# Hymba block on one core: raw weight buffers in two pairs, the last two tokens' rows on the tensor engine, and a rotary half swap by copies

## The chip, the cores and the metric

The kernel runs on one core of one Trainium2 chip. The metric is device time in microseconds (us), the median of several executions. One execution was also profiled; the profile gives every instruction of the engines: TensorE (PE, with its weight loads PEld), VectorE (DVE), ScalarE (ACT), GpSimd (POOL) and SyncE (SP, which here only issues DMAs).

## The reference

The model is one block on 1024 tokens of width 1024, all float32, with 16 learned meta tokens put in front (1040 tokens) and dropped at the end. Eight heads run side by side: four of an mLSTM (heads 0 to 3 in the kernel) and four of a retention (heads 4 to 7). Their mixed output is projected, a residual is added, and a gated MLP with a causal depthwise convolution follows.

```python
def reference(...):
    h = concatenate([meta, x], axis=1)
    h = h + token_mixer(rmsnorm(h, norm_mix_g), w_in, ..., w_out)
    h = h + channel_mixer(rmsnorm(h, norm_ffn_g), w_up, w_gate, ffn_conv_w, w_down)
    return rmsnorm(h, norm_final_g)[:, N_META:]

def rotary(t, pos):
    ...
    t1, t2 = t[..., : d // 2], t[..., d // 2:]
    return concatenate([t1 * cos - t2 * sin, t1 * sin + t2 * cos], axis=-1)

def token_mixer(u, w_in, ..., w_out):
    proj = up @ w_in
    (ml_q, ml_k, ml_v, ml_o, ml_i, ml_f, rt_q, rt_k, rt_v, rt_g) = split(proj)
    # mLSTM: conv + silu on q and k, a chunkwise scan with gates
    # retention: rotary on q and k, a chunkwise scan with fixed decays
    mixed = concatenate([gate(o) * head_norm(h_ml), silu(g) * head_norm(h_rt)])
    return mixed @ w_out
```

## The kernel before

**Tiling.** Activations lie with the features on the 128 partitions and the tokens along the free axis; the residual stream is eight tiles of 128 features by 1040 tokens. Each large product is done in float32r, both operands split into a high part (a rounding copy on ACT) and a low part (a subtraction on DVE), with three matmuls for each product (`mm3s`, lines 675 to 677). On top of that the large products use a Strassen-Winograd scheme with seven instead of eight block products, so the raw weights have to be added and subtracted on DVE before they are split (`quartered`, lines 361 to 385).

**Order of heads.** The mixer works on the heads in the order 4, 0, 1, 2, 3, 5, 6, 7. For each there are projection units: `q` (q and k), `o` (the output gate) and `v` (by pairs of heads, `u_vp`). PE runs these projections back to back. The scan of a head, its norm and its gating (`scan_a`, `scan_b`, `post_steps`) are put between the projection steps of the following heads.

**The order of work.** The program is dealt out in Python. `go` runs through the projection steps of a unit, and `slot` puts up to two pieces of side work from the list `side` behind each. Whether a piece is dealt depends on a running estimate of the engines' load (`load`, filled by `watch`, lines 91 to 105): side work waits while DVE or ACT is ahead of PE by more than 2.5 us. Pieces that stop at a `yield` go on at the next step (`tick`). The instruction order within the engines is then settled by the framework's list scheduler, which works from this order and its own timing estimate. Every engine, and each DMA queue, executes its instructions in order.

**Raw weight buffers.** All raw weights of the mixer pass through four tiles of 128 x 1024 (512 KB each), `raw0` to `raw3`. `job` (line 211) registers a load, and `jload` starts them strictly in the order of registration whenever one of the four slots is free:

```python
while jfreed and len(jraw) < min(len(jobs), jcap[0]):
    i = len(jraw)
    jslot[i] = jfreed.pop(0)
    ...
    nc.sync.dma_start(x[:, o:o + y.shape[1]], y)
```

Users of these slots are of two kinds. The main ones feed PE's projections: `u_load`, `u_fm` (two jobs for each `q` or `o` unit, named for instance `raw_q3a`, `raw_q3b`) and `u_vp` (four jobs). The side ones are:

- `w_unit(k)`: two blocks of `w_out` are combined by four DVE additions (lines 437 to 441) and stored to memory (line 443), as prepared operands for the output projection. Three of the eight come at the very start.
- `v_unit(p, s, r)`: the meta tokens' v, by matmuls in plain float32 on column groups of 32 (line 513, PSUM tile `pvm`), two units for each head.
- `m_unit(h)`: the output projection's contribution of the last two tokens. Those two tokens lie outside the two halves of 512 tokens that the output projection works on. For each head the two blocks of `w_out` rows (`raw_m`) are scaled by the two tokens' values `mm` (lines 414 to 418, ACT and DVE), and the result is accumulated into `accd` in memory (lines 422 and 424, the latter by an accumulating DMA of POOL). At the end (lines 1757 to 1789) `accd` is read back, the last head's share is added (line 1768), and 16 matmuls with a column of ones (line 1787, PSUM tile `pe`) sum over the partitions.
- `first_right(k)`: the mixed rows of the first eight blocks (`raw_fr`, from `mxd`), split and stored again for the first stage of the output projection (lines 479 to 485).

**Rotary.** For the retention heads (lines 919 to 932) two DVE products write each other's half of the partitions (L925, L926: 64 partitions each), a full-width product with the cosines (L928) and an addition (L929) follow. This is done for q and k and for two halves of the tokens. `gates` (lines 937 to 1026) computes the mLSTM gates once; in the side list it comes behind all four rotary pieces of head 4.

**The output projection** is the stage `mixw` (line 1241; steps "1", "65", "73", "4", "2"), with the residual's input loaded at line 1611 behind its second step. From about 742 us on the MLP follows; neither its structure nor the down projection's is touched.

Of the kernel before, what the change touches and what calls it, by code (L numbers as in the profile page):

```python
# [17 lines left out]
P = 128  # L18
# [6 lines left out]
H = 4  # L25
# [40 lines left out]
def body(ctx, tc, h_in, vecs, cst, mask_in, rot, w_v0, w_vp, w_g, w_out, w_up, w_gate, w_down, out):  # L66
# [24 lines left out]
    def watch(ins):  # L91
# [15 lines left out]
    vec = per.tile([P, V_N], F32, name="vec")  # L107
    cs = per.tile([P, C_N], F32, name="cs")
    epsc = per.tile([P, 1], F32, name="epsc")
# [16 lines left out]
    accd = [dram.tile([P, D], F32, name=f"accd{t}") for t in range(2)]  # L126
# [15 lines left out]
    mm = per.tile([P, 2 * 8, 2], F32, name="mm")  # L142
# [31 lines left out]
    AC.dma_start(vec, vecs)  # L174
# [8 lines left out]
    G.memset(gts[:, :, 0, :], 0.0)  # L183

# [20 lines left out]
    jobs = []  # L205
    jraw = {}
    jslot = {}
    jfreed = [0, 1, 2, 3]
# [5 lines left out]

    def jload():
        while jfreed and len(jraw) < min(len(jobs), jcap[0]):
            i = len(jraw)
            nm, srcs = jobs[i]
            jslot[i] = jfreed.pop(0)
            x = jraw[i] = raw_tile(nm, jslot[i])  # L220
            o = 0
            for y in srcs:
                nc.sync.dma_start(x[:, o:o + y.shape[1]], y)
                o += y.shape[1]
# [10 lines left out]

    def jfree(*ids):
        jfreed.extend(jslot[i] for i in ids)
        jload()
# [32 lines left out]
    def busy():  # L271
        return not rush[0] and max(load["DVE"], load["Activation"]) - load["PE"] > 0.5

# [67 lines left out]
    def u_load(key, *srcs):  # L341
        nm = "_".join(str(k) for k in key)
        i = job(nm, *srcs)
# [43 lines left out]
    def u_fm(kind, h, *extra):  # L387
        w = w_g[GI[kind, h]]
        nm = f"{kind}{h}"
        ja = job(nm + "a", w[:, HB:3 * HB])  # L390
        jb = job(nm + "b", w[:, 3 * HB:], w[:, :HB])
# [4 lines left out]
    def u_vp(p):  # L396
        w = w_vp[p]
        js = [job(f"vp{p}_{x}", w[:, WB[x] * UN:(WB[x] + 1) * UN]) for x in ("11", "21", "12", "22")]
        quartered(("vp", p), js, lambda: [jraw.get(j) for j in js], 2, {3: (js[0],), 4: (js[2],), 5: (js[3],), 6: (js[1],)}, f"vp{p}")

    def m_unit(h):
# [3 lines left out]
        def make():  # L405
            assert {k, k + 1} <= posted, k

            def g():
                yield from jwait(*js)
                x0, x1 = (jget(j) for j in js)  # L410
                for j in range(2):
                    y0, y1 = (x[:, j * HB:(j + 1) * HB] for x in (x0, x1))
                    t = st.tile([P, HB], F32, tag="mt", name=f"mt{k}_{j}")
                    AC.activation(t, y0, AF.Copy, scale=mm[:, k, 0:1])
                    AC.activation(y0, y0, AF.Copy, scale=mm[:, k, 1:2])
                    yield
                    V.scalar_tensor_tensor(y0, y1, mm[:, k + 1, 1:2], y0, ALU.mult, ALU.add)
                    V.scalar_tensor_tensor(y1, y1, mm[:, k + 1, 0:1], t, ALU.mult, ALU.add)
                    yield
                for i, x in enumerate((x1, x0)):  # L420
                    if h == 4:
                        nc.sync.dma_start(accd[i], x)
                    else:
                        G.dma_start(accd[i], x, accum_op=ALU.add)
                jfree(*js)
            spawn(g())
        unit(("m", h), 0, make)

    def w_unit(k):
        js = [job(f"w{k + 8 * i}", w_out[k + 8 * i]) for i in range(2)]  # L430

        def make():
            def g():
                yield from jwait(*js)
# [6 lines left out]
                V.tensor_tensor(v12, v12, v11, ALU.add)  # L441
                for x, st_, o in ((v22, "65", HB), (v21, "73", HB), (v11, "65", 0), (v12, "73", 0)):
                    nc.sync.dma_start(sums["w", st_, k][:, o:o + HB], x)
                jfree(*js)
# [24 lines left out]
    def first_right(k):  # L469
        i = job(f"fr{k}", mxd[k])  # L470

        def make():
            assert k in posted, k
            hi, lo = half_tiles(f"fr{k}")

            def g():
                yield from jwait(i)
# [4 lines left out]
                V.tensor_tensor(a[:, HB:], a[:, :HB], a[:, HB:], ALU.subtract)  # L482
                nc.sync.dma_start(rone[k][:, :HB], hi.bitcast(F32))
                nc.sync.dma_start(rone[k][:, HB:], lo.bitcast(F32))
                nc.sync.dma_start(diff[k], a[:, HB:])
                jfree(i)
# [8 lines left out]
    metab = {}  # L495
    posted = set()

    def v_unit(p, s, r):
        o = WB[f"{r + 1}{s + 1}"] * UN
        i = job(f"vm{p}{s}{r}", w_vp[p][:, o:o + UN])  # L500

        def make():
            done.add("meta")

            def g():
                yield from jwait(i)
                while r and ("vm", p, s, 0) not in done:
                    yield
                pv = metab.get((p, s)) or pp(f"pvm{p}_{s}", "tr")
                metab[p, s] = pv  # L510
                y = jget(i)
                for k in range(4):
                    PE.matmul(pv[32 * k:32 * k + 32, :DV], ug[:, 4 * r + k, :], y[:, k * DV:(k + 1) * DV],
                              start=r == 0, stop=r == 1, tile_position=(0, 32 * k))
                jfree(i)
                done.add(("vm", p, s, r))
                if r:
                    yield from quads(vz[:META, s * 264:s * 264 + DV], pv, DV)
# [1702 lines left out]
```

## Time and profile before

| | us |
|---|---|
| median of 3 runs | 1546.32 (1541.36 to 1550.5) |
| the profiled execution, its own time | 1552.62 |
| its span, first to last instruction | 1550.5 |
| TensorE busy in the span | 1494.9 |
| VectorE busy | 1109.5 |
| ScalarE busy | 761.8 |
| GpSimd busy | 85.1 |
| mean granted TensorE clock | 0.98 of full speed |
| DMA traffic | 232.17 MB, mean 150 GB/s |

Times in the trace count from the first instruction. A group's row in the profile has the line, the engine, the operation, what it writes and reads by the program's names, and the count; then busy time and the mean duration of one in ns; then the idle time of the engine just before and what ended it. In a timeline row the start and the duration come first. Matmuls are pipelined, so their durations overlap. The granted clock is that of TensorE; it falls to half when the engine was idle and takes some us to come back.

### The profile page before, as it was taken

The page shows a single profiled execution, that of the slowest core. Times are in us where ns is not written, and L with a number is a line of the kernel's source. Part 1 is how long each engine was busy: PE and PEld are TensorE (multiplying, and loading weights), DVE is VectorE, ACT ScalarE, POOL GpSimd, SP SyncE. Part 2 cuts the span into 40 slices and gives each one's busy share as a digit, 9 for nine tenths or more (in the row PEclk, how much of TensorE's full clock was granted, in tenths as well). Part 3 has the DMA queues.
Part 4 walks back from the last instruction along what each step waited for, and adds up shares of the span by engine and source line. Part 5 has one row for each costly group of instructions (what it writes and reads, how often), then busy time and mean ns, then how long its engine had stood idle before and what let it go on. Part 6 is the DMA issues. An engine that isn't in the chain of part 4 may idle for free.

```text
span 1550.5 us, 25359 instructions
## 1 busy us (share of the span) xinstructions
PE 1494.9 (96%) x9819; PEld 1357.0 (88%) x9819; DVE 1109.5 (72%) x2156; ACT 761.8 (49%) x1459; POOL 85.1 (5%) x144
## 2 busy tenths in 40 slices
PE   6979999998999989989999999999999999999997
PEld 5979999997999988987888998999999999888887
DVE  8886778765877667755787688766666666778656
ACT  5445666745663545454354455444444444434443
POOL 1000000000000000000000001222220000000000
PEclk9989999999999999999999999999999999999998
DMA  7331265325542356498532327887773223933213
GB/s 264 128 110 56 69 203 160 92 77 169 183 112 83 100 190 187 143 306 319 171 125 100 103 85 227 207 215 197 185 190 88 82 82 131 383 104 115 95 42 109
DMA packets 107176, 232.17 MB, mean 150 GB/s; under 512 B 10808, under 2 KB 34048, under 8 KB 106880
## 3 DMA queue, kind: packets, MB, share of 16 engines
q1 hardware_dynamic: 96736, 201.12, 38.9%
q0 software_dynamic: 10176, 29.37, 9.8%
q8 instruction: 77, 1.26, 0.3%
q14 instruction: 43, 0.35, 0.1%
q10 hardware_dynamic: 144, 0.07, 0.0%
HBM read 179.10 MB, written 74.49 MB: 164 GB/s over the span
## 4 chain that ended last, share of the span: by engine, by line
PE 81%; DMA 9%; DVE 7%; ACT 1%; issue 1%; SPq 0%; DVEq 0%; ACTq 0%
PE pdx L675 3%; PE pdx L677 3%; PE pdx L676 3%; PE pup_x L676 2%; PE pup_x L677 2%; PE pup_x L675 2%; PE pga_x L676 2%; PE pga_x L677 2%; PE pga_x L675 2%; PE pdy L675 2%; PE pdy L677 2%; PE pdy L676 2%; PE pwx L676 2%; PE pwx L675 2%; PE pwx L677 2%; DMA accd<-raw_m 2%
## 5 line engine op out<-in xcount | busy, mean ns | idle before, releaser
L575 ACT CAST hi_up<-raw_up 128x512 fp32r<-128x512 f32 (+1 forms) x52 | 36.4, 719 | 107.2 <-PE pga_z L676 60.3
L576 DVE TENSOR_TENSOR lo_ga<-fraw_ga,hi_ga 128x512 fp32r<-128x512 f32 (+1 forms) x52 | 41.9, 808 | 37.7 <-ACT hi_ga L575 37.5
L675 PE MATMUL pup_x<-uh_g,hi_up 128*128 128x256 f32 (+1 forms) x240 | 67.5, 284 | 1.2 <-ACT uh_g L1625 1.2
L676 PE MATMUL pup_x<-ul_g,hi_up 128*128 128x256 f32 (+1 forms) x240 | 67.5, 283 | 0.1
L576 DVE TENSOR_TENSOR lo_up<-raw_up,hi_up 128x512 fp32r<-128x512 f32 (+1 forms) x52 | 41.2, 809 | 35.9 <-ACT hi_up L575 35.1
L677 PE MATMUL pup_x<-uh_g,lo_up 128*128 128x256 f32 (+1 forms) x240 | 66.6, 283 | 0.0
L576 DVE TENSOR_TENSOR lo_d<-rd,hi_d 128x1024 fp32r<-128x1024 f32 (+1 forms) x34 | 37.7, 1113 | 32.9 <-ACT hi_d L575 32.7
L575 ACT CAST hi_ga<-fraw_ga 128x512 fp32r<-128x512 f32 (+1 forms) x52 | 36.4, 718 | 45.8 <-PE pup_z L676 22.9
L677 PE MATMUL pdx<-uh_d,lo_d 128*128 128x512 f32 (+1 forms) x156 | 57.9, 374 | 0.0
L676 PE MATMUL pdx<-ul_d,hi_d 128*128 128x512 f32 (+1 forms) x156 | 57.6, 373 | 0.0
L575 ACT CAST hi_d<-rd 128x1024 fp32r<-128x1024 f32 (+1 forms) x34 | 32.4, 962 | 49.4 <-PE pdy L676 32.6
L677 PE MATMUL pdy<-uh_d,lo_d 128*128 128x512 f32 x132 | 51.7, 392 | 0.0
L676 PE MATMUL pdy<-ul_d,hi_d 128*128 128x512 f32 x132 | 51.3, 389 | 0.0
L675 PE MATMUL pdx<-uh_d,hi_d 128*128 128x512 f32 (+1 forms) x156 | 49.0, 375 | 0.0
L675 PE MATMUL pdy<-uh_d,hi_d 128*128 128x512 f32 x132 | 48.5, 393 | 0.0
L675 PEld LDWEIGHTS pup_x<-uh_g,hi_up 128*128 128x128 f32 x240 | 45.8, 191 | 2.3 <-ACT uh_g L1625 1.4
L676 PE MATMUL pga_x<-ul_g,hi_ga 128*128 128x512 f32 x120 | 47.6, 397 | 0.0
L677 PE MATMUL pga_x<-uh_g,lo_ga 128*128 128x512 f32 x120 | 47.3, 394 | 0.0
L675 PE MATMUL pga_x<-uh_g,hi_ga 128*128 128x512 f32 x120 | 47.3, 394 | 0.0
L676 PEld LDWEIGHTS pup_x<-ul_g,hi_up 128*128 128x128 f32 x240 | 45.8, 191 | 1.1 <-DVE ul_g L1626 0.3
L677 PEld LDWEIGHTS pup_x<-uh_g,lo_up 128*128 128x128 f32 x240 | 44.9, 190 | 0.8
L1260 PE MATMUL s<-qT,kT 128*128 128x128 f32 (+1 forms) x144 | 27.9, 275 | 11.7 <-DVE kT L929 8.7
(1685 smaller groups left out, 5814.9 us busy)
## 6 DMA issues: line engine op xcount, KB each, us to landing
raw_up<-w_up_d SPq DMA_DIRECT2D x22, 512.0 KB, 4.1
fraw_ga<-w_gate_d SPq DMA_DIRECT2D x22, 512.0 KB, 4.3
acts<-cv SPq DMA_DIRECT2D x44, 256.0 KB, 3.4
wsd<-w_down_d POOLq DMA_DIRECT2D x44, 256.0 KB, 6.4
rd<-wsd SPq DMA_DIRECT2D x22, 512.0 KB, 3.4
raw_w<-w_out_d SPq DMA_DIRECT2D x20, 512.0 KB, 5.8
wsw<-raw_w SPq DMA_DIRECT2D x32, 256.0 KB, 2.0
raw_m<-w_out_d SPq DMA_DIRECT2D x14, 512.0 KB, 3.9
```

The source lines that it names most:

```text
L575: AC.copy(hi[:, o:o + n], x)
L576: V.tensor_tensor(lo[:, o:o + n], x, hi[:, o:o + n].bitcast(F32), ALU.subtract)
L675: m.append(PE.matmul(pt, ah, xh_, start=first and k == 0, stop=False, skip_group_check=True))
L676: PE.matmul(pt, ah, xl_, start=False, stop=False, skip_group_check=True)
L677: m.append(PE.matmul(pt, al, xh_, start=False, stop=last and k == n - 1, skip_group_check=True))
L1260: PE.matmul(s[:, :L], k, q, start=True, stop=True)
```

## The change

Four parts, and some smaller edits.

1. *Raw buffers in two pairs.* Slots 0 and 1 serve only the main jobs (`line`), in their order; slots 2 and 3 serve the side jobs, which now ask for their load when they are dealt (`ask`) and proceed when PE's load estimate has advanced by 4 us since the load was issued (`landed`). Of the four jobs of a `v` unit, "11" and "12" are main and "21" and "22" come through the side pair. Stores and frees of side jobs are put later (`lag`). Two of the three `w_unit`s at the start move to the `o` units of heads 1 and 3.
2. *The last two tokens.* `m_unit` no longer scales rows on ACT and DVE. `tail_sum` multiplies the raw `w_out` rows with a 32-column stationary operand (two tokens' values, followed by columns that are not used) in four column groups of 256 columns each, in a PSUM tile `pm` of the tag `tr`, and adds the result to `tail`. The DRAM accumulators, the accumulating DMAs and the column-of-ones matmuls go; at the end two transposes bring `tail` into the residual's layout.
3. *Rotary.* Two ACT copies swap the halves, and one full-width DVE product takes the place of the two half-width ones; the sine table has its signs the other way round.
4. *Order around head 4.* The second pair of rotary pieces comes behind the gates, and the load estimate starts at 4 us for DVE and 2 us for ACT.

The smaller ones: the `v_unit`s of a head become one; column-group matmuls count a quarter of what they did in the load estimate; head 7's score pieces wait while the `tr` bank is in use for meta work, and a scan's first step waits for its head's meta v; the residual's loads come behind the fifth step of `mixw`.

```diff
-            load[nm] += 2 * max(0.11, 2 * n)
+            load[nm] += max(0.11, 2 * n) * (0.5 if ins.outs[0].ap[0][1] == 32 else 2)
...
-    epsc = per.tile([P, 1], F32, name="epsc")
+    epsc = vec[:, V_N:V_N + 1]
...
-    accd = [dram.tile([P, D], F32, name=f"accd{t}") for t in range(2)]
...
-    mm = per.tile([P, 2 * 8, 2], F32, name="mm")
+    mm = per.tile([P, 2 * 16, 2], F32, name="mm")
+    tail = per.tile([P, 2 * P], F32, name="tail")
...
+    G.memset(mm, 0.0)
...
+    def jput(i, side_):
+        nm, srcs = jobs[i]
+        jslot[i] = jfreed[side_].pop(0)
+        age[i] = load["PE"]
+        x = jraw[i] = raw_tile(nm, jslot[i])
...
     def jload():
+        while jfreed[0] and line and len(jraw) < jcap[0]:
+            i = line.pop(0)
+            jput(i, 0)
+            if i in partner:
+                asked.insert(int(bool(asked) and asked[0][0][0] in jraw), (partner[i], False))
+        while jfreed[1] and asked and jcap[0] > 2:
+            ids, slow = asked[0]
+            if slow and line and line[0] in partner and ids[0] not in jraw:
+                break
+            i = next(x for x in ids if x not in jraw)
+            jput(i, 1)
+            if i == ids[-1]:
+                asked.pop(0)
...
+    def landed(us, *ids):
+        yield from jwait(*ids)
+        while dealt[0] and not rush[0] and load["PE"] - max(age[i] for i in ids) < us:
+            yield
...
+    def lag(us):
+        t = load["PE"]
+        while dealt[0] and not rush[0] and load["PE"] - t < us:
+            yield
...
+    def tail_sum(h, rows, free=None):
+        k = 2 * h
+        done.add("meta")
+        pt = pp(f"pm{h}", "tr")
+        for b, x in enumerate(rows):
+            for g in range(4):
+                PE.matmul(pt[32 * g:32 * g + 32, :2 * P], mm[:, k + b:k + b + 16].rearrange("p k t -> p (k t)"), x[:, 2 * P * g:2 * P * (g + 1)],
+                          start=b == 0, stop=b == 1, tile_position=(0, 32 * g))
+        yield
+        if h == HEADS[0]:
+            V.tensor_copy(tail, pt[:, :2 * P])
+        else:
+            V.tensor_tensor(tail, tail, pt[:, :2 * P], ALU.add)
+        done.discard("meta")
+        if free:
+            jfree(*free)
...
     def m_unit(h):
...
-                    AC.activation(t, y0, AF.Copy, scale=mm[:, k, 0:1])
-                    AC.activation(y0, y0, AF.Copy, scale=mm[:, k, 1:2])
...
-                    V.scalar_tensor_tensor(y0, y1, mm[:, k + 1, 1:2], y0, ALU.mult, ALU.add)
-                    V.scalar_tensor_tensor(y1, y1, mm[:, k + 1, 0:1], t, ALU.mult, ALU.add)
...
-                        G.dma_start(accd[i], x, accum_op=ALU.add)
+                ask(js)
+                yield from landed(4, *js)
+                while "meta" in done:
+                    yield
+                yield from tail_sum(h, [jget(j) for j in js], js)
...
-    for f in w_units(3):
+    for f in w_units(1):
...
-        u_fm("o", b, *(v_units(p + 1, 0) if p < 2 else r_units(2, 3)), *m_units(a))
+        u_fm("o", b, *(v_units(p + 1, 0) if p < 2 else r_units(2, 3)), *m_units(a), *w_units(p < 2))
...
-            V.tensor_tensor(t[0:64, a:b], x[64:128, a:b], A2[64:128, a:b], ALU.mult)
-            V.tensor_tensor(t[64:128, a:b], x[0:64, a:b], A2[0:64, a:b], ALU.mult)
+            AC.copy(t[0:64, a:b], x[64:128, a:b])
+            AC.copy(t[64:128, a:b], x[0:64, a:b])
             yield
             V.tensor_tensor(d[:, a:b], x[:, a:b], A1[:, a:b], ALU.mult)
+            V.tensor_tensor(t[:, a:b], t[:, a:b], A2[:, a:b], ALU.mult)
             V.tensor_tensor(d[:, a:b], d[:, a:b], t[:, a:b], ALU.add)
...
-    side += qk_tasks(4) + gate_tasks + scan[:12]
+    side += qk_tasks(4)[:2] + gate_tasks + qk_tasks(4)[2:] + scan[:12]
...
+    load.update({"DVE": 4.0, "Activation": 2.0})
...
-        if t == 1:
+        if t == 4:
             for kb in range(0, KB, 2):
...
-                y = acc[i, j]
-                after(V.scalar_tensor_tensor(y, x[:, b * D + j * HB:b * D + (j + 1) * HB], mm[:, 14 + b, i:i + 1], y, ALU.mult, ALU.add), last["rsplit"][1])
...
         if st == "4" and k == 0:
+            for _ in tail_sum(7, [x[:, b * D:(b + 1) * D] for b in range(2)]):
+                pass
+        if st == "4" and k == 1:
             pe = pp("pe2", "tr")
-            for mb in range(KB):
-                for i in range(2):
-                    PE.matmul(pe[:, 2 * mb + i:2 * mb + i + 1], acc[i, mb // 4][:, mb % 4 * P:(mb % 4 + 1) * P], cs[:, C_M01 + P - 1:C_M01 + P], start=True, stop=True)
+            for j in range(2):
+                PE.transpose(pe[:, j * P:(j + 1) * P], tail[:, j * P:(j + 1) * P], ident)
```

More of the change, by code (lines that the diff above doesn't have):

```diff
@@ L205, in body @@
     jobs = []
+    line = []
+    partner = {}
+    asked = []
     jraw = {}
     jslot = {}
-    jfreed = [0, 1, 2, 3]
+    age = {}
+    jfreed = [[0, 1], [2, 3]]
     jcap = [2]
@@ L213, in job, with main_job, ask @@
         return len(jobs) - 1
-    def jload():
[L216 to L224, printed above, removed]
+    def main_job(nm, *srcs):
+        i = job(nm, *srcs)
+        line.append(i)
+        return i
+    def jput(i, side_):
[3 more added lines that the diff above has]
+        x = jraw[i] = raw_tile(nm, jslot[i])
+        o = 0
+        for y in srcs:
+            nc.sync.dma_start(x[:, o:o + y.shape[1]], y)
+            o += y.shape[1]
+    def jload():
+        while jfreed[0] and line and len(jraw) < jcap[0]:
[11 more added lines that the diff above has]
+                asked.pop(0)
+    def ask(ids, slow=False):
+        asked.append((list(ids), slow))
+        jload()
     def jget(i):
@@ L430, in w_unit @@
         js = [job(f"w{k + 8 * i}", w_out[k + 8 * i]) for i in range(2)]
+        if k == 0:
+            ask(js)
         def make():
             def g():
-                yield from jwait(*js)
+                if k:
+                    ask(js, True)
+                yield from landed(4, *js)
                 r1, r2 = (jget(j) for j in js)
@@ L656, in first_norm @@
             m = AC.copy(parts_[i][0], x)
-            last.setdefault("first", m)
+            if r == 0:
+                last["first"] = m
         for x, (h_, l_) in zip(xs, parts_):
@@ L1026, in gates @@
         done.add("gates")
-    RES, rring, acc = [], [], {}
+    RES, rring = [], []
     HALF = SEQ // 2
@@ L1211, in wdraw @@
         if st == "1" or nm in ("w65_0", "w65_1", "w65_2", "w65_3"):
-            return raw_tile(nm, jfreed.pop(0) if jfreed and st == "1" else None)
+            left = next((q for q in jfreed if q), None)
+            return raw_tile(nm, left.pop(0) if left and st == "1" else None)
         if not wdraws:
```

103 lines of the change are left out of this document (49 added, 54 removed).

## The prediction

> **What bounds the kernel now.** I read the page's first two parts, then the busy time and clock by stretches, then what TensorE (PE) waited for, and last the chain of waits around each stretch found.
>
> ```profile
> PE 1494.9 (96%) x9819; PEld 1357.0 (88%) x9819; DVE 1109.5 (72%) x2156; ACT 761.8 (49%) x1459; POOL 85.1 (5%) x144
> PE   6979999998999989989999999999999999999997
> ```
>
> PE is the bound, with holes in the first half: the mixer. In the windows below, columns are stretch, length, then busy us and instructions of PE, PEld, DVE, ACT, POOL, then the granted clock, the DMA share and GB/s. I count as lost the length less PE busy times clock.
>
> ```profile
> 100.00:116.00 16.00, 7.27 (x42) 6.87 (x41) 13.56 (x28) 3.69 (x8) 0.00 (x0) 0.68 0.20 67
> 224.00:240.00 16.00, 14.99 (x117) 14.05 (x116) 13.21 (x31) 14.54 (x33) 0.18 (x1) 1.00 0.75 239
> 376.00:396.00 20.00, 14.62 (x99) 13.54 (x98) 11.23 (x32) 13.38 (x28) 0.96 (x3) 0.91 0.85 268
> 420.00:430.00 10.00, 9.14 (x69) 7.87 (x68) 6.78 (x14) 5.74 (x13) 0.00 (x0) 1.00 0.56 175
> 540.00:560.00 20.00, 16.04 (x99) 14.89 (x99) 8.78 (x22) 12.00 (x20) 0.00 (x0) 0.83 0.63 195
> 600.00:636.00 36.00, 32.76 (x231) 30.81 (x231) 22.86 (x58) 16.37 (x38) 0.86 (x1) 1.00 0.61 176
> 672.00:698.00 26.00, 21.56 (x134) 19.26 (x133) 9.66 (x27) 12.00 (x25) 1.75 (x2) 0.87 1.04 350
> 712.00:742.00 30.00, 26.58 (x107) 20.29 (x106) 20.09 (x37) 11.17 (x18) 0.00 (x0) 0.89 0.80 288
> ```
>
> Lost: 11.1, 1.0, 6.7, 0.9, 6.7, 3.2, 7.2 and 6.3, together 43.1 us. What ended the larger waits (waiter, awaited, total, times, longest):
>
> ```profile
> PE s L1260 <- DVE kT L929: 8.7, 1, 8.7
> PE pq3x L675 <- ACT hi_o L295: 4.0, 1, 4.0
> PE n L1309 <- ACT n L1322: 3.7, 1, 3.7
> PE pq6x L675 <- ACT hi_o L295: 2.7, 1, 2.7
> ```
>
> Behind three of them the chain of waits shows one pattern: a raw buffer held by side work.
>
> ```profile
> 375.72 9.22 DMA accd<-raw_m
> ...
> 536.76 9.14 DMA accd<-raw_m
> 545.92 5.40 DMA raw_fr<-mxd
> ...
> 673.93 14.77 DMA raw_w<-w_out_d
> ```
>
> And the DMA queue SP issued in between:
>
> ```profile
> 382.82 0.33 SPq L223 DMA_DIRECT2D raw_q3a<-w_g_d  x1
> 384.95 0.33 SPq L223 DMA_DIRECT2D raw_w<-w_out_d  x1
> ...
> 543.59 0.33 SPq L223 DMA_DIRECT2D raw_q6a<-w_g_d  x1
> 545.92 0.32 SPq L223 DMA_DIRECT2D raw_fr<-mxd  x1
> ```
>
> The weights that PE needs next (q3a, q6a) stand in one first-in-first-out line with rows of w_out and of the mixed heads, and buffers come free only when the 9 us accumulation into accd has read them.
>
> **The buffers in two pairs.** Main weights get slots 0 and 1, side jobs 2 and 3. q3a and q6a then wait for the split of the previous main block alone. Does a pair suffice? A projection unit has 14 steps of 12 matmuls, each some 0.12 us behind the last:
>
> ```profile
> 253.24 0.28 PE L675 MATMUL po1x<-uS2h,hi_o 128*128 128x258 f32 x1
> 253.35 0.28 PE L676 MATMUL po1x<-uS2l,hi_o 128*128 128x258 f32 x1
> 253.56 1.07 PE L513 MATMUL pvm<-raw_vm,ug 128*32 128x256 f32 x16
> ```
>
> That is 20 us in all, 2.9 for each of seven products; the slot of block b is given back at its sixth split, emitted at the second of seven products, the next block's first split at the fourth, its first use after the seventh: five products, 14 us, for a load that lands in 5:
>
> ```profile
> raw_q6a<-w_g_d SPq DMA_DIRECT2D x1, 512.0 KB, 5.0
> ```
>
> So I take back 6.0 of the 6.7 at 376 (0.7 for its neighbours' waits on DVE) and all 6.7 at 540; nothing as lower bound, since SP remains one queue and a weight load can still stand behind a store that waits for DVE. The stores and frees now come later in program order (the lags), which shortens SP's waits and lengthens how long side slots are held; only side work waits for those. Two of the three w units at the start move behind PE's stretches of heads 1 and 3: eight DVE adds of 0.68 us, four loads and eight stores. PE has no hole between 50 and 100, so the start gains nothing.
>
> ```profile
> L441 DVE TENSOR_TENSOR raw_w<-raw_w,raw_w 128x512 f32<-128x512 f32 x8 | 5.4, 683 | 0.0
> ```
>
> **The tail rows on PE.** Per head m_unit had 4 ACT scalings, 4 DVE multiply-adds and two accumulations. These go for seven heads, with eight more DVE operations at the end:
>
> ```profile
> L417 DVE SCALAR_TENSOR_TENSOR raw_m<-raw_m,mm,raw_m 128x512 f32<-128x512 f32 x14 | 10.5, 747 | 8.0 <-DMA raw_m<-w_out_d 6.2 <-ACT raw_m L415 1.8
> L414 ACT ACTIVATE mt<-raw_m,mm 128x512 f32<-128x512 f32 x14 | 10.1, 721 | 8.3 <-DMA raw_m<-w_out_d 6.3 <-DVE raw_m L418 1.9
> L1768 DVE SCALAR_TENSOR_TENSOR acc<-wm,mm,acc 128x512 f32<-128x512 f32 x8 | 5.9, 742 | 0.0
> ```
>
> L418 and L415 match L417 and L414, so DVE loses 26.8 us and ACT 20.2. They lay beside PE and are worth nothing by themselves. What comes is eight sums of eight column-group matmuls of 256 columns, of exactly the shape of the pvm products whose 16 records stand at 253.56 above:
>
> ```profile
> L690 DVE TENSOR_TENSOR vz<-pvm,vz x18: 415/419/426, 83.7 to 528.9; 16x256 f32<-16x256 f32 x18
> 833.64 3.46 PE pe L1787 x32
> ```
>
> Eight such matmuls (16 records) take 1.07 us, 1.0 on the path; on a full PE that is +8.0 us, plus 0.3 for two transposes, less the 3.5 of pe: net +4.8 on the path. Eight DVE adds of 0.42 hide where DVE is 56% busy (376 to 396). The group starts 0.21 us after the matmul ahead of it, where matmuls follow each other at 0.11 to 0.12: entering it costs 0.1. The Trainium skill, TensorEngine Tiling (Array Packing), Key Properties, says that a change of tiling mode drains the engine, which speaks against small groups between full matmuls. With that 0.1 at each of 16 changes the +4.8 would be 6.4, an estimate; I leave it out, as it is inside every bound below.
>
> The sums add a real wait: PE itself now waits for w_out's rows, and behind it stand all projections. The landed guard holds a sum back until PE's planned load is 4 us past the issue. The same wait existed for pvm, without a guard:
>
> ```profile
> L513 PE MATMUL pvm<-raw_vm,ug x96: 379/379/404, 78.3 to 526.6; 128*32 128x256 f32 x96
>   issue: 1.0, 4
> ```
>
> PE lost 1.0 us there in all, no DMA named. I take 0 for the sums, with 12 us (seven at the 1.7 us by which the median of raw_m's landings, 5.7, exceeds 4) as upper bound:
>
> ```profile
> DMA to landing us min/median/max: 3.5/5.7/12.2
> ```
>
> **The rotary.** L925 and L926 become ACT copies and one full-width DVE product; gates are dealt ahead of the second half.
>
> ```profile
> 98.04 0.70 DVE L925 TENSOR_TENSOR kT<-rawq,A 64x528 f32<-64x528 f32 x1
> ...
> 109.94 1.28 DVE L929 TENSOR_TENSOR kT<-kT,rawq 128x528 f32<-128x528 f32 x2
> L295 ACT CAST hi_q<-raw_q6a x4: 615/618/621, 550.2 to 561.5; 128x512 fp32r<-128x512 f32 x4
> ```
>
> The first score product of head 4 waited for the first half's last add. Between these rows DVE did eight half-width products (5.6 us); in their place two full ones of 0.7 stand ahead of it: 4.2 less. One add and one product of the second half move behind: 1.3 more. So 5.5 of the 8.7 us wait go. The copies have no row; the nearest, a cast of 512 columns, takes 0.62 us, so 32 copies cost ACT some 20 us, which the departed scalings pay for. At 100 to 116 ACT was busy 3.7 of 16 us, cover enough; without it 2.5 us of copies would go back onto the wait. The 2.3 us that the lower clock cost here I leave in place. The Trainium skill, TensorE: Matmul & The Clock Gate, What's actually happening, has the clock halve only after an idle window of about 3.4 us; by it the shortened wait of 3.2 would cost no clock and 7.8 would be saved. At 540 a wait of 2.7 us did lower the clock to 0.83, against it.
>
> **The other edits.** The residual's loads are issued three steps later (t = 4), behind some loads of weights and mixed rows that they now precede on SP. The load at 673.93 took 14.77 us amid a DMA share of 1.04; with accd's traffic and the residual's eight loads out of its way I take about half that (raw_m's rows, of the same size, land in 5.7), and PE's wait of 3.7 with its ramp goes: 5.0 of 7.2; nothing if the other loads fill DMA anyway. The residual's first reader is late enough, at 730.5, even for 14.8 us:
>
> ```profile
> L1171 DVE TENSOR_TENSOR resid<-resid,pwx x4: 681/683/689, 730.5 to 732.9; 128x512 f32<-128x512 f32 x4
> ```
>
> At 600 PE waited for DVE, which itself waited for the mixed heads' rows:
>
> ```profile
> DVE raw_fr L482 <- DMA raw_fr<-mxd: 13.5, 4, 5.1
> ```
>
> With their own slots loaded earlier half of the 3.2 goes, 1.5. Of 1.0 + 0.9 at 224 and 420, 1.0. The 6.3 at 712 are the scan's end and stay. The memset of mm on POOL (5% busy), epsc inside vec, the gates' two stores reaching SP earlier and the changed load figures cost nothing on the path.
>
> **Sum.** Back: 5.5 + 6.0 + 6.7 + 1.5 + 5.0 + 1.0 = 25.7. Added: 4.8. The order of all engines is laid anew, and with less slack elsewhere a removed stall uncovers the next (DVE's split of the same block, late by 1 to 3 us): I put 4.4 in, two thirds of one stall like that at 540, bounds 0 and 13.4 (two). Net -16.5. The profiled execution took 1552.6 (span 1550.5), 6.3 above the median of runs, 1546.3; so 1536 for a profiled one and **1530** against the median. Its own range: all but the 712 stall gone, -36.8 + 4.8, 1514; halves of 376, 540 and 672 back and 13.4 of new stalls, 1548.
>
> **The rivals.**
> 1. More goes: DVE's 35 us less (26.8, and 11.1 for the rotary's 16 products of 0.7, less 3.4 for the sums' adds) lets the scan and the 712 stretch follow too: -36.8 - 3 + 4.8, 1511. For: DVE 13.6 of 16 busy at 100. Against: at 672 DVE was busy 9.7 of 26, idle already.
> 2. The stalls stay because SP stays one queue, or because two main slots are too few: only rotary, 600 and the small ones are gained, -8.0 + 4.8, 1543. For: raw_q3a was issued right before a raw_w in one queue. Against: the 14 us margin.
> 3. Slower: each sum stops PE until its w_out rows land. At 4.2 us each (wait plus half clock) seven sums cost 29: 1546.3 - 20.9 + 29.4 = 1555; it decides from 3 us each, when the whole gain is gone. For: landings up to 12.2. Against: pvm.
>
> **How the numbers follow.** Forecast 0.46, rival 1 0.2, rival 2 0.18, rival 3 0.11, rest 0.05. Range 1512 to 1552: it leaves out rival 1's better half, and rival 3 above 1552, together some 0.2. Half a percent, 7.7 us, is what a measurement can tell: faster is under 1538.6. Of the forecast 0.42, all of rival 1 and 0.08 of rival 2 lie there, 0.70; slower, over 1554, are rival 3's 0.11 and 0.04 of the rest and the forecast's tail; 0.15 between.
>
> **What would show it.** Right: no accd, mt or acc; pm groups near 1.0 us, PE busy time up about 5 us; the wait of s on kT near 3; raw_q3a and raw_q6a issued without a store's landing before them, no wait of pq3x and pq6x; the first raw_w load after 660 under 10 us; DVE some 35 us less. Wrong: PE idle in front of pm on raw_m; new waits on hi or lo of a q, v or o block; a wait on resid; mixer stretches still losing over 30 us.

## The result, and the profile after

The changed kernel took 1547.35 us (median of 12 runs, 1543.38 to 1549.96) against 1545.99 for the kernel before on the same chip (1541.36 to 1550.5): ratio 1.0011, 95% interval 0.9996 to 1.0026. That is no change that can be measured, where 1530 was forecast. The profiled execution has a span of 1546.4 (1550.5 before).

The page's first lines, after:

```profile
PE 1497.8 (97%) x9917; PEld 1353.0 (87%) x9917; DVE 1080.8 (70%) x2112; ACT 766.1 (50%) x1464; POOL 74.3 (5%) x133
PE   6999799999999999999999999999999999999997
```

DVE lost 28.7 us of work (35 forecast), PE gained 2.9 (5 forecast). The windows of the prediction (without 420), with three more where the trace shows new holes (columns as before):

```profile
100.00:116.00 16.00, 16.00 (x130) 15.42 (x129) 11.79 (x31) 8.35 (x17) 0.00 (x0) 1.00 0.21 67
160.00:178.00 18.00, 9.58 (x42) 7.28 (x41) 15.54 (x36) 14.58 (x25) 0.11 (x1) 0.73 0.07 25
224.00:240.00 16.00, 12.14 (x82) 11.58 (x83) 10.45 (x29) 12.86 (x26) 0.18 (x1) 0.89 0.46 146
312.00:320.00 8.00, 6.40 (x40) 6.14 (x41) 6.82 (x16) 7.97 (x19) 0.18 (x1) 0.79 0.00 0
376.00:396.00 20.00, 20.00 (x169) 17.94 (x168) 12.13 (x40) 9.84 (x25) 0.75 (x3) 1.00 0.62 183
396.00:408.00 12.00, 8.92 (x57) 8.35 (x56) 7.15 (x14) 9.76 (x17) 0.00 (x0) 0.86 0.46 147
540.00:560.00 20.00, 20.00 (x163) 17.28 (x163) 12.63 (x35) 9.30 (x23) 0.00 (x0) 1.00 0.34 104
600.00:636.00 36.00, 35.95 (x269) 33.44 (x268) 25.75 (x65) 21.21 (x47) 0.00 (x0) 1.00 0.52 174
672.00:698.00 26.00, 26.00 (x195) 23.42 (x194) 12.09 (x32) 14.03 (x32) 0.00 (x0) 1.00 1.04 392
712.00:742.00 30.00, 26.45 (x113) 20.48 (x112) 16.83 (x31) 8.88 (x14) 0.00 (x0) 0.94 0.67 230
```

By the prediction's measure (length less PE busy times clock) the old holes at 100, 376, 540, 600 and 672 went from 34.9 us together to 0.1; 712 still loses 5.1. In their place stand 11.0 at 160, 5.2 at 224 (1.0 before), 2.9 at 312 and 4.3 at 396 (0.1 at most in each of the other three before). PE's waits name what ends them (waiter, awaited, total, times, longest; a wait on `sig`, `rawk` or `rawq` is one for an evacuation, the copy of a finished result out of PSUM, the memory that matmuls write):

```profile
PE tr L1421 <- ACT v4lo L1412: 3.8, 1, 3.8
PE tr L1421 <- DVE mx L1429: 3.4, 2, 2.6
PE pq1y L729 <- ACT sig L795: 2.0, 1, 2.0
PE pq2x L729 <- DVE rawk L799: 1.9, 1, 1.9
PE pq3y L729 <- ACT sig L795: 1.8, 1, 1.8
```

Between 60 and 760 us no wait over 0.7 us is for the split of a raw buffer any more. The 3.8 and the 2.6 of the first two rows lie in the hole at 160: the transposes `tr` of head 4's normed rows. Head 4's scan ran late, and no long wait of PE shows why. The timeline of PE shows, before, the first score tiles `s` (the first after the 8.7 us wait), then the gates' tiles `pe`, `pf`, `pt`:

```profile
110.67 0.61 PE L1260 MATMUL s<-qT,kT 128*128 128x16 f32 x2 [8.73 <-DVE kT L929]
116.28 0.49 PE L1260 MATMUL s<-qT,kT 128*128 128x128 f32 x2
120.65 0.19 PE L986 MATMUL pe<-cs,gates 36*1 36x36 f32 x1
126.12 0.41 PE L1005 MATMUL pf<-gsm,cs 1*128 1x36 f32 x2
132.70 0.38 PE L1024 MATMUL pt<-cs,gates 36*128 36x36 f32 x3
136.16 0.38 PE L1260 MATMUL s<-qT,kT 128*128 128x128 f32 x2
```

And after, where the gates' `pe` had been at 104.0 and 106.9 and `pf` at 112.2, the first `s` comes behind the last of the gates' tiles and behind their reader on DVE (`cols`):

```profile
122.41 0.25 PE L1080 MATMUL pt<-cs,gates 36*128 36x36 f32 x1
127.22 0.40 PE L1317 MATMUL s<-qT,kT 128*128 128x16 f32 x2 [0.47 <-DVE cols L1081]
```

`s` and the gates' four tiles (`pg`, `pe`, `pf`, `pt`) are allocated from one PSUM tag, `sA`. Tiles of one tag share its buffers, and `sA` has one: whoever is given out first holds it until its reader is done. In the kernel after, all four gates tiles were used ahead of the first `s`, and the scan began 16.5 us later. PE's projections of that stage ran on without it (100 to 116 is full). From 161 to 174 us PE has only steps of this scan and of its norm to do, and waits between them. That the shared buffer is the reason is so far an argument; e5 tests it.

### The profile page after: what moved, and what is told of

It reads as the page before. It is cut to its first block, busy times and chain, and to the rows that moved or that the text cites. A ratio compares the mean times of both kernels' runs of the same rounds, so it can differ in the third digit from the quotient of the medians.

```text
span 1546.4 us, 25487 instructions
## 1 busy us (share of the span) xinstructions
PE 1497.8 (97%) x9917; PEld 1353.0 (87%) x9917; DVE 1080.8 (70%) x2112; ACT 766.1 (50%) x1464; POOL 74.3 (5%) x133
## 4 chain that ended last, share of the span: by engine, by line
PE 80%; DVE 4%; DMA 4%; ACT 3%; issue 1%; SPq 0%; DVEq 0%; ACTq 0%
PE pdx L731 3%; PE pdx L730 3%; PE pdx L729 3%; PE pup_x L730 2%; PE pup_x L731 2%; PE pga_x L729 2%; PE pup_x L729 2%; PE pga_x L730 2%; PE pga_x L731 2%; PE pdy L731 2%; PE pdy L730 2%; PE pdy L729 2%; PE pwx L731 2%; PE pwx L729 2%; PE pwx L730 2%; PE n L1366 2%
## 5 line engine op out<-in xcount | busy, mean ns | idle before, releaser
L509 POOL DMA_DIRECT2D wsd<-w_down_d x33 | 19.7, 733 | 471.6 <-DVE s2up L1916 471.2
```

What stands on the lines that cost most here:

```text
L509: dep(G.dma_start(x, y), last["pace"], True)
```

## The experiments

Each run lists its time and its ratio to the kernel before on the same chip, with the 95% interval. The four groups below ran on four chips, so a difference of two runs from different groups carries both intervals, some 2 to 3 us each.

**Four first runs: which part makes the holes.** The gates' place and the start's load offset undone in the kernel after (e1); the lag ahead of the tables' loads taken out of it (e2); the kernel before with the gates' place and the offset alone (e3); the kernel before with the rotary by copies alone (e4).

```diff
 e1, after
-    side += qk_tasks(4)[:2] + gate_tasks + qk_tasks(4)[2:] + scan[:12]
+    side += qk_tasks(4) + gate_tasks + scan[:12]
-    load.update({"DVE": 4.0, "Activation": 2.0})
 e2, after
-            yield from lag(3)
             tables_load(h)
 e3, before: e1's lines the other way round
 e4, before
-            V.tensor_tensor(t[0:64, a:b], x[64:128, a:b], A2[64:128, a:b], ALU.mult)
-            V.tensor_tensor(t[64:128, a:b], x[0:64, a:b], A2[0:64, a:b], ALU.mult)
+            AC.copy(t[0:64, a:b], x[64:128, a:b])
+            AC.copy(t[64:128, a:b], x[0:64, a:b])
...
+            V.tensor_tensor(t[:, a:b], t[:, a:b], A2[:, a:b], ALU.mult)
...
```

> The changed kernel with part 4 undone: all four rotary pieces ahead of the gates again, and no start value for the load estimate. Theory A (pile-up): the wait that appeared at 160 to 178 us comes from head 4's scan starting 17 us later (first n product at 133 instead of 117 us), so that it ends when the products of v0 need head 4's tiles. Then the first n comes near 118, the 160 to 178 stretch loses under 3 us instead of 11.6, and of the old 8.7 us wait near 102 some 3 to 5 us come back: 4 to 8 us less than the changed kernel. Theory B (the new wait comes from the buffers in two pairs or the rotary on ScalarE): it stays within 2 us of 8.4 us of waits, and the time is equal or up to 8 us more, since the wait at 102 comes back as well.

> The changed kernel, only the decay tables' loads are dealt at once again instead of 3 us of TensorE load later. Theory A (late tables): the three new stalls at 224, 312 and 396 (9.3 us of waits, 12.8 us lost with the clock) come from eight exponentials and two table loads of ScalarE standing ahead of the evacuations of po and pq; with earlier tables the waits fall under 4 us and the time by 6 to 9 us. Theory B (they come from the order of the scheduler or the buffers): waits and time stay within 2 us.

> The kernel before with part 4 alone (second rotary half behind the gates, load estimate starting at 4 and 2 us). Theory A: the 8.7 us wait near 102 goes or falls under 2 us, and a new wait of 6 us or more appears between 150 and 185, where the v0 products need head 4's tiles; the time stays within 4 us of before. Theory B: only the old wait goes: 8 to 11 us less.

> The kernel before with the rotary half swap by ScalarE copies alone. Theory A (the wait near 102 is VectorE's queue): eight half-width products become four full ones, 2.8 us less ahead of the last add in all, so the wait of 8.7 falls to 5 to 6 and the time by 3 to 5 us. Theory B (other VectorE work moves into the gap, or the copies stand in ScalarE's way): wait and time stay within 1.5 us.

e1: 1549.66, ratio 1.0012 (0.9999 to 1.0025); the hole at 160 stays, the first `s` comes at 126.7. e2: 1549.83, 1.0017 (1.0003 to 1.0032); the four waits on ACT and DVE stay. So in the kernel after neither the place of the gates in the list nor that lag makes the holes by itself, and the first theory fell. e3: 1555.75, 1.0053 (1.0034 to 1.0072): on the kernel before the new order alone costs 8 us. PE now waits in front of `pe`:

```profile
PE pe L986 <- DVE gates L979: 8.2, 1, 8.2
```

That wait stands where the 8.7 for `kT` had been, so it is not the loss. The first `s` comes at 133.0, behind all of the gates, and PE loses more further on, among others 2.8 at 160 to 178 and 3.1 at 396 to 408 (0.0 and 0.1 before). Where all of the 8 us went was not followed.

e4: 1550.65, 1.0006 (0.9986 to 1.0025). The wait that the rotary was to shorten did fall from 8.7 to 4.4, and the time stayed:

```profile
PE pq6x L675 <- DVE sig L745: 5.5, 1, 5.5
PE pq1x L675 <- ACT hi_q L295: 4.7, 1, 4.7
PE s L1261 <- DVE kT L930: 4.4, 1, 4.4
```

New or longer waits further on stand against the gain: in this trace all later work lies in another order.

**The bank, the order, or the load figures.** In e5 only the tag of the gates' tiles is changed; in e6 the gates are given out behind the first four scan pieces; e7 puts back the load figure of the column-group matmuls, which has a part in when the scan is given out; e8 puts the new figure alone into the kernel before.

```diff
 e5, after (the same for pe, pf, pt)
-        pg = ps.tile([P, 512], F32, tag="sA", bufs=1, name="pg")
+        pg = ps.tile([P, 512], F32, tag="tr", bufs=1, name="pg")
 e6, after
-    side += qk_tasks(4)[:2] + gate_tasks + qk_tasks(4)[2:] + scan[:12]
+    side += qk_tasks(4) + scan[:4] + gate_tasks + scan[4:12]
 e7, after; e8, before, the other way round
-            load[nm] += max(0.11, 2 * n) * (0.5 if ins.outs[0].ap[0][1] == 32 else 2)
+            load[nm] += 2 * max(0.11, 2 * n)
```

> The kernel after, with the four PSUM tiles of the gates (pg, pe, pf, pt) in the bank tr in place of sA, which the score tiles s of the scan use; instructions, order and emission are those of after. In after the gates' four tiles stand ahead of head 4's first score tile in the single bank sA, the first s starts at 127.2 and the first n at 133.4, and PE loses 11.6 us at 160 to 178. Theory C (the bank's order delays head 4's scan and so makes the new stall): first s at 108 or earlier, first n before 117, the loss at 160 to 178 at most 4, time 6 to 12 under after, 1535 to 1541. Rival D (the dealer gives out the scan too late because pvm and pm count a quarter in its load figures; the bank has no part): first n stays at 128 or later, the loss stays at 9 to 13, time within 3 of after. Rival E (head 4's scan does not fit ahead of the reuse of its v tiles in any order): first n may come earlier, the loss at 160 to 178 stays near 11, time within 3 of after.

> The kernel after, with the gates given out behind the first four pieces of head 4's scan instead of between the two halves of its rotary; banks are those of after. Theory C: first s at 106 or earlier, first n before 118, the loss at 160 to 178 at most 4, time 1535 to 1542, unless head 0, which needs the gates, now waits (its tables then come later: stretch 178 to 236). Rival D: the same for the first s, since the scan is given out at step 7 in place of 14, so this run parts C and D from E only. Rival E: the loss of about 11 stays, time within 3 of after.

> The kernel after, with the load figure of fp32 matmuls of 32 output partitions back at that of before (four times the new one); only the order in which side work is given out changes. The first scan piece is then given out at step 9 in place of 14, two steps of the gates still unfinished. Theory C: the scan is partly interleaved with the gates in bank sA: first n between 118 and 130, the loss at 160 to 178 between 4 and 9, time 3 to 7 under after. Rival D: the loss at 160 goes, and with it the ones at 224, 312 and 396 (4.9, 3.1 and 4.8 in after), time 10 to 20 under after. Rival E: time within 3 of after, loss at 160 stays near 11.

> The kernel before, with the new load figure for fp32 matmuls of 32 output partitions (a quarter of the old) and nothing else. Its first scan piece is then given out at step 15 in place of 5, behind all of the gates. Theory C: the first s comes at 122 or later (110.7 in before), the wait of s on kT at 102 goes, a stall of 7 to 12 us shows at 160 to 178 that before does not have, time 0 to 8 above before. Rival E: no loss above 3 at 160 to 178, since before's other parts are kept, and the time within 3 of before. D expects as C does here, with further losses at 224 to 400.

e5: **1535.37**, 0.9914 (0.9897 to 0.9930). With the same number of instructions on every engine, the first `s` starts at 100.4, and the scan runs between the gates' tiles:

```profile
100.44 0.29 PE L1317 MATMUL s<-qT,kT 128*128 128x16 f32 x2
100.82 0.19 PE L1042 MATMUL pe<-cs,gates 36*1 36x36 f32 x1
107.57 0.19 PE L1043 MATMUL pe<-cs,gsm 36*1 36x36 f32 x1
107.69 0.49 PE L1317 MATMUL s<-qT,kT 128*128 128x128 f32 x2
...
113.74 0.41 PE L1061 MATMUL pf<-gsm,cs 1*128 1x36 f32 x2
...
119.17 0.37 PE L1080 MATMUL pt<-cs,gates 36*128 36x36 f32 x3
119.47 0.49 PE L1317 MATMUL s<-qT,kT 128*128 128x128 f32 x2
```

Nothing but the tag was changed, so the shared buffer is what held the scan up. The stretch that lost 11.0 is full (windows of e5):

```profile
160.00:178.00 18.00, 18.00 (x139) 16.68 (x138) 11.93 (x29) 6.59 (x16) 0.57 (x3) 1.00 0.24 73
```

The waits of `pq1y`, `pq2x` and `pq3y` stay (2.3, 1.9 and 1.8 us), and with them losses of 2.3 at 216 to 224, 3.4 at 296 to 312 and 3.1 at 376 to 396, 8.8 in place of the 12.4 at 224, 312 and 396: the granted clock is 1.00 in these stretches now. D and E said that the hole and the time would not move, and fall with this run. e6: 1545.82, 0.9983 (0.9971 to 0.9994): the first `s` comes at 100.8, but the later ones still take turns with the gates, PE waits 3.3 us for an evacuation in 160 to 178, and 4.6 are lost there; C's 1535 to 1542 promised too much. e7: 1549.96, 1.0010 (1.0000 to 1.0021): by the dealing the scan is given out five steps earlier, but it does not start earlier, and still stands behind the gates' last tile:

```profile
L1317 PE MATMUL s<-qT,kT x144: 177/273/377, 127.7 to 705.1; 128*128 128x128 f32 x128, 128*128 128x16 f32 x16
```

That agrees with the bank and is against D; C's own 3 to 7 us for partial interleaving were a miss. e8: 1555.52, 1.0043 (1.0024 to 1.0062); the first `s` comes at 134.4, as C said, behind the gates' last tile:

```profile
130.64 0.37 PE L1024 MATMUL pt<-cs,gates 36*128 36x36 f32 x3
134.36 0.29 PE L1260 MATMUL s<-qT,kT 128*128 128x16 f32 x2
```

So in the kernel before the load figure alone turns the order in the bank over, and so does part 4 alone (e3); in the kernel after, taking back either one leaves it turned (e1, e7). Of the 7 to 12 expected at 160 to 178 only 2.3 came, and PE still waits 8.2 us at 102, now for the gates, as in e3. A late scan is therefore not enough for a hole of 11; what else it took in the kernel after was not tried.

**Is it the change's gain, and whose.** e9 puts the gates into `tr` in the kernel before. e10 to e12 each undo one part of the change in e5: the rotary (e4's lines back), the sums (rows scaled on ACT and DVE and accumulated in DRAM, by the lines of before, but from the side pair), and part 4 (e1's lines).

> The kernel before, with the four PSUM tiles of the gates in the bank tr in place of sA; order and instructions are those of before. Asks whether the 12 us that this edit gave on the kernel after belong to the change or were to be had all along. Theory C (the change's own order made the mask): in before the gates' tiles already alternate with the scan's, the first s waits for kT at 102 and not for the bank, and the stalls at 376, 540 and 672 lie elsewhere; time within 4 under before, 1544 to 1548, the wait of s on kT still 7 to 10. Rival F (the bank costs both kernels alike): 8 to 12 under before, about 1537, and then the change itself is worth nothing.

> The kernel after with the gates in the bank tr (1535.4 so far), and the rotary of before: two half-width products on DVE in place of two copies on ACT and a full-width product. Prediction's term: the copies save 4.2 of the 5.5 us at 102, so 3 to 6 longer, 1538 to 1541, with a wait of s on kT of 3 to 8 us at about 100. Rival: the copies are worth nothing once the gates are given out ahead of the second half and the start has slack, within 2 of 1535.

> The kernel after with the gates in the bank tr (1535.4 so far), and the last two tokens' rows summed as before: ACT scalings, DVE multiply-adds and accumulation in DRAM, from the side pair of buffers, with the 32 small products at the end; the pairs and all else stay. Prediction's term: the sums on PE cost 4.8 net and never wait, so 3 to 6 shorter, 1529 to 1532. Rival G (the 9 us accumulations hold the side pair so long that pvm, which stops PE, or the mixed heads' rows come late, and 47 us more of DVE and ACT work delay the evacuations at 216, 308 and 384): 3 to 12 longer, 1538 to 1547, with waits of pvm on raw_vm or larger waits on sig and rawk.

> The kernel after with the gates in the bank tr (1535.4 so far), the gates given out behind both halves of the rotary as in before, and the start's load offset (4 and 2) taken out. Theory C: with the banks apart the gates' place no longer matters to the scan; the scan is given out at step 9 in place of 14; within 3 of 1535, first s before 106. Rival (the order itself, not the bank, carries the gain at 102): the first s waits for kT again by 3 us or more, 1538 to 1542.

e9: 1552.02, 1.0024 (1.0007 to 1.0040): no gain on the kernel before, whose old waits stay:

```profile
PE s L1260 <- DVE kT L929: 7.6, 1, 7.6
PE pq6x L675 <- ACT hi_o L295: 4.6, 1, 4.6
```

So the gain of e5 is the change's, hidden in the kernel after by the bank. e10: 1539.67, 0.9942 (0.9922 to 0.9962), 4.3 us above e5, where the copies were given 4.2. The size agrees, the path does not: the wait for `kT` that was to come back with 3 to 8 us is small, and the loss lies in several stretches.

```profile
PE s L1316 <- DVE kT L984: 0.9, 1, 0.9
```

e12: 1541.92, 0.9955 (0.9940 to 0.9971), 6.5 above e5. The first `s` starts at 102.1 without a wait for kT, but a hole comes at 132 (`u` waits 4.2 us for `kw` on ACT), so with the banks apart the new order, with its load offset, does carry a gain; C's "no matter" was wrong.

e11: 1552.99, 1.0034 (1.0012 to 1.0055), 17.6 above e5, beyond even rival G's 12. The waits of `pq3x` and `pq6x` on hi stay away, so it does not take the new sums to remove those. What comes is on DVE and ACT:

```profile
PE tr L1417 <- DVE mx L1425: 7.4, 5, 3.7
PE u L1360 <- DVE C L1373: 6.7, 2, 3.5
PE u L1360 <- ACT kw L1329: 4.6, 1, 4.6
```

These are steps of the scans and of the norms behind them. Part 2 was worth far more than the PE time that its sums cost. How much of it is the two engines' time, how much the accumulations' traffic and how much the side buffers held longer, this run does not part. The parts do not add up either: undone one at a time they cost 4.3, 6.5 and 17.6, together 28.4, while e5 lies 13.0 under the kernel before on its chip.

**What is left.** Four edits of e5: without the lag ahead of the sigmoids (e13); without any of the change's lags (e14); the residual's loads at t = 1 (e15); the gates behind the first four scan pieces (e16, e6's line).

```diff
 e13 and e14
-            yield from lag(1.5)
             AC.activation(sigt[:, b], sigt[:, b], AF.Sigmoid if h < H else AF.Silu)
 e14 also: the lags of tables_load, w_unit (1.5 and 4) and first_right (1.5 and 3)
 e15
-        if t == 4:
+        if t == 1:
```

> The kernel after with the gates in the bank tr (1535.4), without the lag of 1.5 us of planned PE time ahead of each sigmoid. If the lag makes the sigmoids stand ahead of the evacuations at 216 and 384: those stalls (1.7 and 2.6 lost) go, 1531 to 1533. If they come from the chain of the table's DMA, mask, eight exponentials and table loads: they stay, within 2 of 1535.

> The kernel after with the gates in the bank tr (1535.4), without any of the change's lags: sigmoids, table loads, the stores of w and mixed heads, and their frees follow at once. If the lags are what keeps SP clear for the main loads: waits of pq or pv tiles on hi come back, 3 to 8 longer. If the two pairs alone do that, and the lags make the small stalls: 2 to 5 shorter, 1530 to 1533. If neither: within 2.

> The kernel after with the gates in the bank tr (1535.4), with the residual's eight loads issued at t = 1 as in before. Prediction's term: 5.0 us of stall at 672 come back, 1538 to 1541, with a first raw_w load of 10 us or more there. Rival (the stall of before came from the accumulations in DRAM and the order of loads, the residual's loads hide anyway): within 2 of 1535.

> The kernel after with the gates in the bank tr (1535.4), and the gates given out behind the first four pieces of head 4's scan. Theory C (the bank was all of it): the place no longer matters, within 3 of 1535. If giving the scan out at step 7 in place of 14 gains by itself: 1530 to 1532. If the gates' lateness holds up head 0's tables: 2 to 7 longer, with the loss at 200 to 230 grown.

e15: 1534.93, 0.9920 (0.9905 to 0.9936), the time of e5: the residual's loads hide at both places. e13: 1530.78, 0.9891 (0.9872 to 0.9910), and e14: **1530.03**, 0.9891 (0.9873 to 0.9908), the fastest of all, 4.9 under e15 on the same chip: the sigmoids' lag costs 4 to 5 us, the other lags nothing that can be told. No wait of `pq` or `pv` on hi comes back in e14, so the lags are not what keeps those away. e16: 1538.25, 0.9941 (0.9921 to 0.9961), some 3 slower than e5, with a wait of 2.4 us for an evacuation at 104.

Why the lag costs is open. ACT's timeline in e5, at the hole of 216, where `pq1y` waits for the evacuation at 220.16:

```profile
211.31 2.45 ACT L938 ACTIVATE A<-A,cols 128x128 f32<-128x128 f32 x8 [1.46 <-DVE A L932]
213.78 1.28 ACT L1402 ACT_TABLE_LOAD   x1
...
217.90 1.28 ACT L838 ACT_TABLE_LOAD   x1
219.20 1.06 ACT L838 ACTIVATE sig<-sig 128x1026 f32<-128x1026 f32 x1
220.16 0.63 ACT L795 COPY sig<-po0x 128x256 f32<-128x256 f32 x2
```

Eight exponentials of the decay table, a reload of the function table, a sigmoid of 1.06 us, and only then the evacuation that PE needs. Without the lag the same list stands there 1.8 us earlier, and the wait is 1.6 in place of 2.3. But the other wait that was to go, at 384, stays too, and the holes are hardly smaller: of the 4.4 us by which e13's span is shorter than e5's, PE's idle time (span less busy time, 41.2 and 40.2) gives 1.0. The other 3.4 are PE's busy time (1492.5 to 1489.1), with the same 9917 matmuls. ACT runs four reloads of the function table less, of 1.28 us each. How that would shorten PE's busy time is not shown, so the time came as the theory of the evacuations said, but not by its path.

Two main and two side slots against one shared pool was not tried by itself.

## Why the prediction was wrong

**Right.** The old stalls: the windows at 376, 540, 600 and 672 are full in the kernel after, all 23.8 us of them, where I took 19.2. The loads of `raw_q3a` and `raw_q6a` are issued at 367.3 and 536.5 (382.8 and 543.6 before), as the pairs were to do; the pairs by themselves were not run, but these stalls stay away without the new sums (e11) and without the lags (e14) too. The rotary's copies: 4.2 of the 5.5 are theirs, the wait for `kT` shrinks by 4.3 in e4 and the time by 4.3 between e10 and e5, but no run shows both at once. The sums' time on PE: eight groups of 16 records, 1.07 us as read from `pvm`, and no wait of `pm` on `raw_m`, so rival 3 did not come. Rival 2's 1543 is the number nearest to the measured one, by luck: its stalls are the ones that went. The one group at the end, and what is left of `pe` there:

```profile
829.68 1.07 PE L447 MATMUL pm<-wm,mm 128*32 128x256 f32 x16
838.22 0.38 PE L1843 MATMUL pe<-cs,tail 128*128 128x128 f32 x2
```

**Right in sum, wrong in cause.** For 672 I named the residual's loads beside accd's traffic. e15 shows nothing for the loads. With the accumulations back, and the scalings with them (e11), PE loses 3.1 at 688:

```profile
688.00:696.00 8.00, 6.14 (x33) 5.50 (x31) 3.58 (x9) 3.69 (x10) 0.00 (x0) 0.79 1.03 379
```

**The step that failed** is the term for what follows from the new order: "a removed stall uncovers the next [...]: I put 4.4 in [...], bounds 0 and 13.4". It took some 16 to 20, and not by a stall that was uncovered. Of these 12 to 15 are the bank `sA` (12.0 by the medians of the kernel after and e5, 15 by their ratios 1.0011 and 0.9914), and 4 to 5 the sigmoids' lag. Both lay in the full diff. Two sentences of the prediction put the bank at nothing. The step "gates are dealt ahead of the second half" was priced by the DVE work ahead of `kT` alone, and "the changed load figures cost nothing on the path". Each of the two alone, the first with its load offset, moves the scan behind all of the gates in the kernel before and costs 7 to 8 us there (e3, e8); I did not ask which PSUM buffer the gates take and who is next for it. And the lags had a price only for how long they hold side slots ("only side work waits for those"); the one ahead of the sigmoids had no term. By what path it costs stays open.

Without both, and without the other lags (e14), the kernel takes 1530, 16.4 under the kernel before, where the forecast had 16.5. That the terms add up so closely is luck, as e15 and the next term show.

**A second wrong term** is that of the sums, +4.8, with the sentence that DVE's 26.8 and ACT's 20.2 us "lay beside PE and are worth nothing by themselves". With the bank mended, going back to the scalings and accumulations loses 17.6 (e11): in that kernel the term had the wrong sign and was 22 us off. The waits that come with it are for DVE and ACT; which of the things that e11 puts back makes them stays open.

**What stays open.** The windows' holes (without 420) fell from 42.2 to 28.7 us together, the span by 4.1 only. Of the 9.4 between, the sums explain 5.5 (8 x 1.07 + 0.38 - 3.46), and 2.2 is a new hole in the MLP; the rest lies in no single stretch and was not followed.

```profile
888.00:900.00 12.00, 10.31 (x75) 9.75 (x74) 8.40 (x24) 4.28 (x10) 0.00 (x0) 0.95 0.06 23
```

## What to carry to other kernels

When a change alters the order in which work is given out, list for each moved piece the single-buffered tiles that it takes, PSUM first, and who allocates from them next: an order fixed there can show as late work without a long wait, and a comparison of start times between the two traces finds it. Price the wait, and then the stage that has to absorb the late work. If a change of this kind brings nothing, take the suspected shared buffer away before undoing its parts: here four runs that undid or added parts told little, and one new tag gave back most of what was missing.

## What the runs showed of the hardware

The length of a wait alone did not decide whether the granted clock fell. In the kernel after, PE waited once for 1.9 us, up to 313.6, with no other wait from 300 us on, and the clock was 0.50 from 315 to 318 while PE worked. In e5 it waited 2.3 us, up to 220.6, and the clock stayed at 1.00:

```profile
315.00:318.00 3.00, 3.00 (x16) 2.77 (x14) 2.41 (x6) 2.99 (x11) 0.18 (x1) 0.50 0.00 0
218.00:224.00 6.00, 3.74 (x29) 3.37 (x28) 4.67 (x9) 5.42 (x9) 0.00 (x0) 1.00 0.51 181
```

The low clock came late and cost work: in 160 to 178 of the kernel after PE was idle for 8.4 us, in waits of 3.8 us at most, and the granted clock of 0.73 on the mean added 2.6 us to them. The prediction laid the clock of 0.83 at 540 to one wait of 2.7 us. The trace of before has two, of 2.7 and 1.2 us with 1.3 us of work between them; the clock was still 1.00 at 547 to 551 and fell to 0.50 (553 to 557) only with the second.
